# Key and value pieces of a dilated attention: two of eight multiplied on VectorE from PSUM instead of on GpSimd, and the second softmax's transposes placed two quarters later

## The chip, the core and the metric

The kernel runs on one core of a Trainium2 chip. The metric is device time in microseconds (us) of one execution.

## What is computed

One inference step of a two-layer decoder (one convolution layer, one attention layer, an MLP behind each) on 256 prompt tokens and 8 sequences of 8 sampled tokens, all in fp32. The attention layer has three head groups with (window, dilation) of (128, 1), (512, 4) and (2048, 16); the sampled tokens also read a key-value cache of 2048 past positions. Cut to the part that matters:

```
def dilated_group_sample(q, k_cat, v_cat, n_past, window, dilation):
    idx = n_past + jnp.arange(S)[:, None] - dilation * jnp.arange(n_keys)[None, :]
    kg = k_cat[:, idx_c]
    vg = v_cat[:, idx_c]
    s = jnp.einsum('bshe,bsnhe->bhsn', q, kg)
    ...
    p = jnp.exp(s - lse)
    o = jnp.einsum('bhsn,bsnhe->bshe', p.astype(vg.dtype), vg)

def merge_groups(outs, lses, dtype):
    w = jax.nn.softmax(jnp.stack(lses), axis=0)
    return jnp.sum(w[..., None] * jnp.stack(outs), axis=0).astype(dtype)
```

With dilation 16 each sampled query has 16 cached keys of its own that it shares with no other query of its sequence, so its scores and its weighted sum of values are not a matrix product with a shared operand: they are a product element by element and a sum.

## The kernel before

**Weights.** Every fp32 weight tile is loaded by SP into a ring `raw` and split into two fp32r halves: ScalarE copies the high part (`wh`, line 126), VectorE subtracts to get the low part (`wl`, line 127). `mm3` then issues three matmuls of 128x320 for each 128x128 weight block (lines 146 to 148). A split makes half of a raw tile, 128x1024; splits are emitted three halves ahead of the matmuls that use them, and the ring of halves has four places.

**The attention stage** is one list of steps that is sorted by a position. The unit is a quarter: twelve matmuls of 128x320. One head's query, key and value projections take 36 quarters, and this is called a frame; frame h holds `qkv_steps(h)` (the projections of head h), `scores2(h)` (its dilation-16 keys) and `side(h - 1)` (everything else of the attention of head h-1). After the eight heads comes one more frame, in which `side(7)` runs beside the first half of the output projection (`wo_steps`). The stage runs from about 1340 to 2200 us. The order of each engine's instructions is the order of that list: an instruction whose input is late holds all behind it on its engine. The second part of a step with a TensorE part (its `post`) is emitted after the next TensorE step.

**The dilation-16 pieces.** Keys and values of one head are each eight pieces of 128x1024 (one per sequence). `piece` places three things: the transfer into one of four buffers `al` at 2.9 quarters ahead, GpSimd's work at its position (a broadcast of one row `R` to all partitions, line 643, and a multiply, line 644) and VectorE's sum over it (line 649) 4.5 quarters later. The rows come from `row`, four small transfers (line 661). Key pieces stand 2.2 quarters apart from position 9 of their frame, value pieces from position 26.6, so the latter run over into the next frame.

**The two softmaxes.** `side` handles prompt rows in two halves: `p_s` makes scores, takes the maximum `mx` (line 753) and normalises (lines 618 to 620, the last two a reciprocal on VectorE and a scaling on ScalarE), `p_t` transposes the result on TensorE (line 761), `p_o` multiplies with the values. For sampled rows `s_soft` takes the maximum `mn` (line 821), and `s_t` and `n_t` transpose (lines 829 and 842). The transposes, the value transposes `v_t`, the scores `new_s` and some others each take one of three PSUM buffers named `s` for a moment; the sample's output product has the one buffer `o`.

## Time and profile before

| | |
|---|---|
| median of three executions | 3119.97 us (3115.67 to 3120.29) |
| the profiled execution | 3116.45 us, span 3114.7 us |
| TensorE, VectorE, ScalarE, GpSimd busy over the span | 95%, 63%, 43%, 27% |
| attention stage, one frame with side work | 97 to 98 us |
| in such a frame: TensorE, VectorE, GpSimd busy | 87, 88 and 74 us |

The shares over the whole span hide what the stages are like: GpSimd's pieces all lie in the attention stage, and VectorE, idle a third of the time elsewhere, is busy there for some nine tenths. Matmuls overlap, so that TensorE's busy time in a stretch is the time in which at least one is under way.

### The profile page before, as it was taken

How to read it: one execution, taken by the hardware profiler on the slowest of the kernel's cores; microseconds unless marked ns; L12 is line 12 of the kernel's file. 1: busy time of each engine (PE TensorE's matmuls, PEld its weight loads, DVE VectorE, ACT ScalarE, POOL GpSimd, SP SyncE). 2: the span in 40 equal slices, each digit the busy share in tenths (PEclk: the TensorE clock that was granted, in tenths of full speed). 3: DMA queues.
4: the chain of work that ended last, by engine and by line, in shares of the span. 5: the costliest groups of instructions: out<-in, count | busy, mean ns of one | idle time of the engine just before them, and what ended most of it. 6: DMA issues, size and time to landing. Idle time of an engine off the chain costs nothing.

```text
span 3114.7 us, 47460 instructions
## 1 busy us (share of the span) xinstructions
PE 2960.2 (95%) x19600; PEld 2897.2 (93%) x19608; DVE 1950.0 (63%) x2258; ACT 1341.0 (43%) x1889; POOL 828.7 (27%) x469
## 2 busy tenths in 40 slices
PE   6999799999999999999898898988999999999998
PEld 6998799999999999999888888877999999999998
DVE  7988854444444444567998888988644444444444
ACT  7877644334334334434334443334532333433442
POOL 2767200000000000034787777876100000000000
PEclk9999899999999999999999999999999999999999
DMA  5443244444444444466776667765444444444442
GB/s 189 146 139 122 96 149 150 150 151 152 152 151 151 149 149 149 149 211 213 260 260 240 253 234 259 257 235 207 146 151 150 149 149 149 149 149 149 149 149 88
DMA packets 96521, 533.62 MB, mean 171 GB/s; under 512 B 13809, under 2 KB 21233, under 8 KB 43825
## 3 DMA queue, kind: packets, MB, share of 16 engines
q1 hardware_dynamic: 92624, 526.54, 48.3%
q10 hardware_dynamic: 3600, 3.57, 0.3%
q8 instruction: 153, 2.51, 0.3%
q14 instruction: 64, 0.52, 0.0%
q0 software_dynamic: 80, 0.49, 0.0%
HBM read 517.33 MB, written 12.70 MB: 170 GB/s over the span
## 4 chain that ended last, share of the span: by engine, by line
PE 80%; DVE 10%; ACT 4%; issue 3%; POOL 2%; DMA 1%; SPq 0%; DVEq 0%; ACTq 0%; POOLq 0%
PE mm L148 25%; PE mm L146 25%; PE mm L147 25%; DVE wl L127 5%; ACT wh L126 1%; PE o L859 1%; POOL al L644 1%; DVE tv L649 1%; POOL pacc L378 1%; DMA al<-v 1%; DVE tk L649 0%; PE mm L368 0%; PE s L774 0%; POOL al L643 0%; ACT prod L377 0%
## 5 line engine op out<-in xcount | busy, mean ns | idle before, releaser
L127 DVE TENSOR_TENSOR wl<-raw,wh 128x1024 fp32r<-128x1024 f32 (+1 forms) x852 | 1213.8, 1431 | 727.2 <-ACT wh L126 727.1
L126 ACT ACTIVATE wh<-raw 128x1024 fp32r<-128x1024 f32 (+1 forms) x852 | 895.0, 1054 | 1478.2 <-PE mm L147 1298.5
L146 PE MATMUL mm<-bh,wh 128*128 128x320 f32 x3200 | 999.3, 312 | 11.9 <-ACT wh L126 11.9
L148 PE MATMUL mm<-bh,wl 128*128 128x320 f32 x3200 | 992.0, 310 | 13.6 <-DVE wl L127 13.5
L147 PE MATMUL mm<-bl,wh 128*128 128x320 f32 x3200 | 990.4, 310 | 0.0
L146 PE MATMUL mm<-ah,wh 128*128 128x320 f32 x2896 | 899.6, 311 | 32.7 <-ACT wh L126 12.6
L148 PE MATMUL mm<-ah,wl 128*128 128x320 f32 x2896 | 897.0, 310 | 3.8 <-DVE wl L127 3.7
L147 PE MATMUL mm<-al,wh 128*128 128x320 f32 x2768 | 855.2, 309 | 7.7 <-DVE al L154 4.0
L148 PEld LDWEIGHTS mm<-bh,wl 128*128 128x128 f32 x3200 | 605.1, 189 | 18.5 <-DVE wl L127 17.7
L146 PEld LDWEIGHTS mm<-bh,wh 128*128 128x128 f32 x3200 | 606.2, 189 | 16.3 <-ACT wh L126 12.2
L147 PEld LDWEIGHTS mm<-bl,wh 128*128 128x128 f32 x3200 | 605.9, 189 | 3.1
L146 PEld LDWEIGHTS mm<-ah,wh 128*128 128x128 f32 x2896 | 547.2, 189 | 39.1 <-ACT wh L126 14.4
L148 PEld LDWEIGHTS mm<-ah,wl 128*128 128x128 f32 x2896 | 547.1, 189 | 6.3 <-DVE wl L127 5.6
L147 PEld LDWEIGHTS mm<-al,wh 128*128 128x128 f32 x2768 | 521.1, 188 | 10.8 <-DVE al L157 5.4
L644 POOL TENSOR_TENSOR al<-al 128x1024 f32<-128x1024 f32 x128 | 360.7, 2818 | 96.2 <-DMA al<-k 50.4
L643 POOL PARTITION_BROADCAST al<-R x128 | 239.3, 1869 | 119.0 <-DMA R<-qT 89.8
L540 POOL DMA_DIRECT2D cb<-cb x1 | 0.7, 682 | 1011.7 <-PE mm L148 1011.7
L1016 POOL TENSOR_TENSOR bh<-bh,r 128x640 f32<-128x640 f32 x2 | 4.2, 2140 | 903.2 <-ACT r L1013 903.2
L378 POOL TENSOR_TENSOR pacc<-pacc,prod 128x320 f32<-128x320 f32 x168 | 181.0, 1113 | 76.0 <-ACT prod L377 75.1
L514 DVE TENSOR_TENSOR x<-x,mm 128x320 f32<-128x320 f32 x128 | 62.4, 487 | 178.8 <-PE mm L148 178.8
L509 DVE SCALAR_TENSOR_TENSOR sg<-mm,r 128x320 f32<-128x320 f32 x126 | 61.8, 492 | 162.4 <-PE mm L148 162.1
L388 DVE SCALAR_TENSOR_TENSOR s<-bl,wdw,s 128x320 f32<-128x320 f32 x272 | 130.0, 545 | 0.4 <-DMA out_cp<-gl 0.3
(205 smaller groups left out, 1715.0 us busy)
## 6 DMA issues: line engine op xcount, KB each, us to landing
raw<-w SPq DMA_DIRECT2D x252, 1024.0 KB
raw<-qkv SPq DMA_DIRECT2D x72, 1024.0 KB
raw<-pw SPq DMA_DIRECT2D x32, 1024.0 KB
al<-k SPq DMA_DIRECT2D x64, 512.0 KB
al<-v SPq DMA_DIRECT2D x64, 512.0 KB
raw<-k SPq DMA_DIRECT2D x16, 1024.0 KB
raw<-v SPq DMA_DIRECT2D x16, 1024.0 KB
raw<-pw2b SPq DMA_DIRECT2D x12, 1024.0 KB
```

The source lines that it names most:

```text
L126: act.activation(wh[:, :n], r, AF.Copy)
L127: dve.tensor_sub(wl[:, :n], r, wh[:, :n])
L146: pe.matmul(ps, wh, xh, start=start, stop=False)
L147: pe.matmul(ps, wh, xl, start=False, stop=False)
L148: pe.matmul(ps, wl, xh, start=False, stop=stop)
L378: pool.tensor_add(pa, pa, pr_)
L388: dve.scalar_tensor_tensor(a, win(f, k), dw(f, k), a, op0=OP.mult, op1=OP.add)
L509: dve.scalar_tensor_tensor(t, ps, 0.0, norm.r, op0=OP.max, op1=OP.mult)
L514: dve.tensor_add(x[:, ob], x[:, ob], ps)
L643: pool.partition_broadcast(wide, E2[kind, h, b // 4][32 * (b % 4):32 * (b % 4) + 1, :])
L644: pool.tensor_mul(t, t, wide)
L649: dve.tensor_reduce(E2["sum", kind, h][:, 8 * b:8 * b + 8], t.rearrange("p (a c) -> p a c", a=8), axis=AX.X, op=OP.add)
```

## The change

Pieces 2 and 5 of the eight (`BY_PE`) no longer go to GpSimd. Their row is sent as two rows, a high and a low part in fp32r; TensorE multiplies them with a 2x128 block of ones (two matmuls of 128x512, line 655 of the changed kernel), which spreads their sum to 128 partitions of two `s` buffers, and VectorE multiplies the piece by each (two 128x512 instructions, line 659). VectorE's total follows 1.5 quarters after the piece's position instead of 4.5. The other six pieces stand 2.9 quarters apart (2.6 in the last head) instead of 2.2 (2.1). A piece is fetched 3.6 quarters ahead, or right after the total that frees its buffer.

To have high and low parts, the query and the softmax weights get one ScalarE copy and one VectorE subtraction more per head. The mask of `new_s` is added by a matmul, and ScalarE copies the result, where VectorE added the mask. Positions in `side` move: `p_t` of the second half from 13.6 and 13.9 to 15.6 and 15.9, behind `s_t` and `n_t`; both `p_o`, `pv`, `s_red` and `s_out` 0.4 to 1.5 later; the `v_t` one quarter apart instead of 0.3.

```diff
+        BY_PE = (2, 5)
...
+            ends.append(at + (1.5 if b in BY_PE else 4.5))
+            j = 32 * (b % 4)
...
+            def on_pe(c):
+                box = {}
+
+                def go():
+                    box["ps"] = ps = s_tile()
+                    pe.matmul(ps, onesr[j:j + 2], E2[kind, h, b // 4].bitcast(F32R)[j:j + 2, 512 * c:512 * c + 512],
+                              start=True, stop=True)
+
+                def post():
+                    dve.tensor_mul(t[:, 512 * c:512 * c + 512], t[:, 512 * c:512 * c + 512], box["ps"])
+                add(at + .3 * c, go, post)
...
-            add(at - 2.9, None, fetch)
-            add(at, None, mult)
-            add(at + 4.5, None, total)
+            add(max(at - 3.6, ends[n - 4] + .01 if n > 3 else 0), None, fetch)
+            if b in BY_PE:
+                on_pe(0)
+                on_pe(1)
+            else:
+                add(at, None, mult)
+            add(ends[n], None, total)
+
+        def pieces(kind, h, t0, dt):
+            i = 0
+            for b in range(NB):
+                piece(kind, h, b, t0 + dt * (i - .5 if b in BY_PE else i))
+                i += b not in BY_PE
...
+                if b in BY_PE:
+                    sp.dma_start(r[32 * j:32 * j + 1, :], hi[8 * b:8 * b + 8, :].bitcast(F32))
+                    sp.dma_start(r[32 * j + 1:32 * j + 2, :], lo[8 * b:8 * b + 8, :].bitcast(F32))
+                else:
+                    sp.dma_start(r[32 * j:32 * j + 1, :], src[8 * b:8 * b + 8, :])
...
-            for b in range(NB):
-                piece("k", h, b, t0 + 9 + 2.2 * b)
+            pieces("k", h, t0 + 9, 2.9)
...
+                    pe.matmul(ps[:64, :NNEW], idb[:, :64], cb[:, B_MN:B_MN + NNEW], start=True, stop=False)
...
-                    dve.tensor_add(S[:, NKEY:], E["new"][:64, :NNEW], cst[:64, C_MN:C_MN + NNEW])
-                    dve.tensor_reduce(E["m"][:, 0:1], S[:, NKEY:], axis=AX.X, op=OP.max)
+                    act.activation(S[:, NKEY:], E["new"][:64, :NNEW], AF.Copy)
+                    dve.tensor_reduce(E["m"][:, 0:1], E["new"][:64, :NNEW], axis=AX.X, op=OP.max)
...
+            def weights():
+                p = E["S"][:, NPE:NKEY]
+                ph = ap.tile([64, 128], F32R, name="qT")
+                pl = ap.tile([64, 128], F32R, name="ql")
+                split_in(ph, pl, p)
...
-                v_t(.3 * g, g)
+                v_t(g, g)
...
-            p_t(6.4, 0, 0)
+            p_t(6.8, 0, 0)
...
-            p_t(13.6, 1, 0)
-            p_t(13.9, 1, 3)
             s_t(14.6, 0, 5)
             n_t(14.9)
-            p_o(17, 1)
-            t2, dt = (13.5, 2.1) if last else (26.6, 2.2)
...
+            p_t(15.6, 1, 0)
+            p_t(15.9, 1, 3)
+            p_o(18.5, 1)
+            step(12.5 if last else 22, None, weights)
+            step(13 if last else 30, None, lambda: row("v", h, 1, *E2["p", h]))
+            pieces("v", h, t0 + (14.5 if last else 26.4), 2.6 if last else 2.9)
```

Two places of the order show what this does around the second softmax of a full frame. First TensorE, before the change: the second `p_t` (line 761, six transposes of `Sp` in two PSUM buffers), one quarter, then `s_t` (line 829) and `n_t` (line 842). `mm` rows are the projections; the bracket names the engine whose work the instruction waits for.

```order
L761 MATMUL s<-cst,Sp 128x128 [waits Activation_49]
L761 MATMUL s<-cst,Sp 128x128 x2
L761 MATMUL s<-cst,Sp 128x128 [waits DVE_49,PE_49]
L761 MATMUL s<-cst,Sp 128x128 x2
...
L829 MATMUL s<-cst,S 128x64 [waits DVE_49]
L829 MATMUL s<-cst,S 128x64 x4
L842 MATMUL s<-cst,S 64x64 [waits Activation_49]
L842 MATMUL s<-cst,S 64x64 x2
```

The same place on TensorE in the changed kernel: first the two spreading matmuls of key piece 2 (line 655), a quarter, `s_t` (line 864) and `n_t` (line 877), a quarter, and then the second `p_t` (line 796).

```order
L655 MATMUL s<-R,ones 128x512 [waits DMAHW6_49,DMAHW5_49]
L655 MATMUL s<-R,ones 128x512 [waits DVE_49]
...
L864 MATMUL s<-cst,S 128x64 [waits Activation_49]
L864 MATMUL s<-cst,S 128x64 x4
L877 MATMUL s<-cst,S 64x64 [waits DVE_49]
L877 MATMUL s<-cst,S 64x64 x2
...
L796 MATMUL s<-cst,Sp 128x128 [waits Activation_49]
L796 MATMUL s<-cst,Sp 128x128 x2
L796 MATMUL s<-cst,Sp 128x128 [waits DVE_49]
L796 MATMUL s<-cst,Sp 128x128 x2
```

`p_t` has moved behind `n_t`, and `n_t`, which waited for ScalarE, now waits for VectorE: of the three `s` buffers it gets the one that the first spreading matmul of line 655 filled, which VectorE's multiply of line 659 empties.

Next VectorE before the change, from the sample's maximum `mn` on: two splits (`wl`), the second softmax's `mx` and reciprocal, the total of a value piece (`tv`), a finished projection (`v`), the head before's output (`os`, `ah`), and the total of a key piece (`tk`).

```order
L821 TENSOR_REDUCE mn<-m 64x1 [waits DVE_49]
L619 RECIPROCAL l<-l 64x1 [waits Activation_49]
L127 TENSOR_TENSOR wl<-raw,wh 128x1024 [waits DMAHW1_49,PE_49,Activation_49]
L753 TENSOR_REDUCE mx<-o 128x1 [waits PE_49]
L619 RECIPROCAL l<-l 128x1 [waits Activation_49]
L649 TENSOR_REDUCE tv<-al 128x8 [waits Pool_49]
L127 TENSOR_TENSOR wl<-raw,wh 128x1024 [waits PE_49,Activation_49]
...
L886 TENSOR_TENSOR os<-os,tv 128x64 [waits DVE_49]
L154 TENSOR_TENSOR ah<-os,ah 128x64 [waits Activation_49]
L649 TENSOR_REDUCE tk<-al 128x8 [waits Pool_49]
L127 TENSOR_TENSOR wl<-raw,wh 128x1024 [waits DMAHW2_49,PE_49,Activation_49]
```

And the same stretch of VectorE in the changed kernel.

```order
L665 TENSOR_REDUCE tv<-al 128x8 [waits Pool_49]
L856 TENSOR_REDUCE mn<-m 64x1 [waits DVE_49]
L620 RECIPROCAL l<-l 64x1 [waits Activation_49]
L127 TENSOR_TENSOR wl<-raw,wh 128x1024 [waits DMAHW7_49,PE_49,Activation_49]
L788 TENSOR_REDUCE mx<-o 128x1 [waits PE_49]
L620 RECIPROCAL l<-l 128x1 [waits Activation_49]
L127 TENSOR_TENSOR wl<-raw,wh 128x1024 [waits PE_49,Activation_49]
...
L154 TENSOR_TENSOR ah<-os,ah 128x64 [waits Activation_49]
L665 TENSOR_REDUCE tk<-al 128x8 [waits Pool_49]
L659 TENSOR_TENSOR al<-al,s 128x512 [waits DMAHW3_49,PE_49]
L127 TENSOR_TENSOR wl<-raw,wh 128x1024 [waits DMAHW0_49,Activation_49]
L659 TENSOR_TENSOR al<-al,s 128x512 [waits PE_49]
```

The total `tv` has moved from behind the second reciprocal to ahead of `mn`, and the two multiplies of key piece 2 stand behind `tk` and around the next split; the first of them also waits for the transfer of its piece.

## Rows read from the trace of the kernel before

**Rows 1.** The page: busy time of each engine over the span, and GpSimd's line of the 40 slices of the span (a slice is 77.9 us, a digit its busy share in tenths).

```profile
PE 2960.2 (95%) x19600; PEld 2897.2 (93%) x19608; DVE 1950.0 (63%) x2258; ACT 1341.0 (43%) x1889; POOL 828.7 (27%) x469
...
POOL 2767200000000000034787777876100000000000
```

**Rows 2.** Busy time by stretch: the frame of the first side work, the next frame, and a stretch of the last head. Columns: the stretch, its length, busy us and instructions of each engine, granted clock, DMA share, GB/s.

```profile
1423.00:1509.00 86.00, 83.75 (x563) 80.15 (x562) 73.25 (x68) 41.13 (x57) 57.59 (x24) 1.00 0.75 269
1515.00:1612.00 97.00, 86.94 (x555) 81.29 (x555) 87.68 (x77) 39.76 (x57) 73.80 (x32) 0.96 0.68 245
...
2122.00:2172.00 50.00, 39.46 (x242) 35.95 (x240) 41.26 (x44) 22.14 (x30) 37.03 (x16) 0.91 0.61 232
```

**Rows 3.** TensorE's timeline, the scores of the new keys (line 713), which stand at position 2.4 of each frame with side work. Columns here and in every timeline: start, duration, engine, line, operation, out<-in, shape, count, and in brackets the idle time before and what ended it.

```profile
1423.25 0.56 PE L713 MATMUL s<-k,q 128*64 128x64 f32 x6
1509.07 0.56 PE L713 MATMUL s<-k,q 128*64 128x64 f32 x6
...
2093.35 0.45 PE L713 MATMUL s<-k,q 128*64 128x64 f32 x4 [4.14 <-DVE q L941]
```

**Rows 4.** The waits of all engines from 1515 to 2121 us (six frames): total, times, longest.

```profile
POOL al L644 <- DMA al<-k: 47.2, 15, 7.4
...
DVE wl L127 <- ACT wh L126: 37.0, 34, 2.5
...
PE s L761 <- ACT Sp L620: 30.1, 6, 5.4
...
POOL al L644 <- DMA al<-v: 23.7, 8, 4.1
...
PE mm L148 <- DVE wl L127: 13.9, 12, 1.7
```

**Rows 5.** VectorE's timeline through the sample softmax and the second prompt softmax of one frame.

```profile
1635.18 0.14 DVE L821 TENSOR_REDUCE mn<-m 64x1 f32<-64x4 f32 x1
1636.58 0.15 DVE L619 RECIPROCAL l<-l 64x1 f32<-64x1 f32 x1 [1.26 <-ACT S L618]
1638.85 1.39 DVE L127 TENSOR_TENSOR wl<-raw,wh 128x1024 fp32r<-128x1024 f32 x1 [2.12 <-ACT wh L126]
...
1642.17 0.16 DVE L619 RECIPROCAL l<-l 128x1 f32<-128x1 f32 x1 [1.06 <-ACT Sp L618]
1642.25 1.20 DVE L649 TENSOR_REDUCE tv<-al 128x8 f32<-128x1024 f32 x1
1644.28 3.08 DVE L127 TENSOR_TENSOR wl<-raw,wh 128x1024 fp32r<-128x1024 f32 x1 [0.83 <-ACT wh L126]
...
1648.93 1.21 DVE L649 TENSOR_REDUCE tk<-al 128x8 f32<-128x1024 f32 x1
```

**Rows 6.** TensorE's timeline over the same stretch.

```profile
1638.05 0.31 PE L147 MATMUL mm<-bl,wh 128*128 128x320 f32 x1
1638.20 0.31 PE L148 MATMUL mm<-bh,wl 128*128 128x320 f32 x1
1643.36 1.22 PE L761 MATMUL s<-cst,Sp 128*128 128x128 f32 x6 [4.85 <-ACT Sp L620]
...
1645.17 0.47 PE L146 MATMUL mm<-bh,wh 128*128 128x320 f32 x1
1645.43 0.47 PE L147 MATMUL mm<-bl,wh 128*128 128x320 f32 x1
...
1649.18 0.35 PE L842 MATMUL s<-cst,S 64*64 64x64 f32 x3 [1.18 <-ACT Sp L764]
```

**Rows 7.** Groups of instructions by line and shape, 1440 to 2121 us (seven frames). Columns: line, engine, operation, out<-in, shapes, count | busy us, mean ns of one | idle before, and what ended it.

```profile
L127 DVE TENSOR_TENSOR wl<-raw,wh 128x1024 fp32r<-128x1024 f32 x194 | 384.5, 2003 | 42.0 <-ACT wh L126 42.0
L644 POOL TENSOR_TENSOR al<-al 128x1024 f32<-128x1024 f32 x112 | 314.7, 2810 | 92.3 <-DMA al<-k 47.8 <-DMA al<-v 24.5 <-DVE wl L127 6.0
...
L859 PE MATMUL o<-wl,zz 128*128 128x512 f32 x70 | 22.2, 398 | 0.0
...
L866 DVE TENSOR_TENSOR Sp<-o,cst 128x1024 f32<-128x1024 f32 x7 | 8.4, 1207 | 0.0
...
L811 DVE TENSOR_TENSOR S<-s,S 64x512 f32<-64x512 f32 x7 | 4.9, 694 | 0.2
...
L811 DVE TENSOR_TENSOR S<-s,S 64x128 f32<-64x128 f32 x8 | 2.3, 293 | 0.2
```

**Rows 8.** The same view for 2230 to 2400 us, where GpSimd does nothing (its slices in the page): the same split.

```profile
L127 DVE TENSOR_TENSOR wl<-raw,wh 128x1024 fp32r<-128x1024 f32 x49 | 60.0, 1225 | 60.8 <-ACT wh L126 60.8
```

**Rows 9.** VectorE's and GpSimd's timelines over one stretch: four splits in a row, and the pieces that GpSimd worked on meanwhile.

```profile
1713.74 9.27 DVE L127 TENSOR_TENSOR wl<-raw,wh 128x1024 fp32r<-128x1024 f32 x4 [0.51 <-ACT wh L126]
...
1711.99 2.41 POOL L644 TENSOR_TENSOR al<-al 128x1024 f32<-128x1024 f32 x1
...
1716.73 3.10 POOL L644 TENSOR_TENSOR al<-al 128x1024 f32<-128x1024 f32 x1
...
1722.16 3.11 POOL L644 TENSOR_TENSOR al<-al 128x1024 f32<-128x1024 f32 x1
```

**Rows 10.** The last head: first and last of GpSimd's sixteen instructions on its value pieces, and TensorE's longest wait from 2121 to 2205 us (total, times, longest).

```profile
2132.17 1.29 POOL L643 PARTITION_BROADCAST al<-R  x1 [17.91 <-DVE x L967]
...
2168.19 2.35 POOL L644 TENSOR_TENSOR al<-al 128x1024 f32<-128x1024 f32 x1
...
PE s L761 <- ACT Sp L620: 6.0, 1, 6.0
```

More of the change, by code (lines that the diff above doesn't have):

```diff
@@ L69 @@
 C_SEL = 192
-C_MN = 200
-C_N = C_MN + NNEW
+C_N = 200
 B_ID = 0
@@ L74 @@
 B_MP = B_MS + NPE
-B_N = B_MP + 1152
+B_MN = B_MP + 1152
+B_N = B_MN + NNEW
 CV_TAPS = {14: (11, 12), 15: (11, 12)}
@@ L541, in decoder_step @@
         idb = cb[:, B_ID:B_ID + 128]
+        onesr = ones.bitcast(F32R)
         B = {}
@@ L628, in decoder_step @@
         E2 = {}
-        slots = [0]
+        ends = []
+        BY_PE = (2, 5)
         def piece(kind, h, b, at):
-            n = slots[0]
-            slots[0] += 1
+            n = len(ends)
             t = spread[:, n % 4]
+            ends.append(at + (1.5 if b in BY_PE else 4.5))
+            j = 32 * (b % 4)
             def fetch():
@@ L650, in total, with row @@
                                   axis=AX.X, op=OP.add)
-            add(at - 2.9, None, fetch)
-            add(at, None, mult)
-            add(at + 4.5, None, total)
-        def row(kind, h, half, src):
+            add(max(at - 3.6, ends[n - 4] + .01 if n > 3 else 0), None, fetch)
[10 more added lines that the diff above has]
+                i += b not in BY_PE
+        def row(kind, h, half, src, hi, lo):
             r = E2[kind, h, half] = ap.tile([128, 1024], F32, name="R", bufs=2)
@@ L670, in post @@
                 q = ap.tile([64, 128], F32, name="qT")
-                act.activation(q, E2["qT", h][:64, :128], AF.Copy)
-                E2["q", h] = q
-                row("k", h, 0, q)
+                qh = ap.tile([128, 128], F32R, name="orr")
+                ql = ap.tile([64, 128], F32R, name="ql")
+                ps = E2["qT", h][:64, :128]
+                act.activation(q, ps, AF.Copy)
+                split_in(qh[:64], ql, ps)
+                E2["q", h] = q, qh[:64], ql
+                row("k", h, 0, *E2["q", h])
             add(t0 + 6, go, post)
-            add(t0 + 12, None, lambda: row("k", h, 1, E2["q", h]))
-            for b in range(NB):
-                piece("k", h, b, t0 + 9 + 2.2 * b)
+            add(t0 + 12, None, lambda: row("k", h, 1, *E2["q", h]))
+            pieces("k", h, t0 + 9, 2.9)
         def side(h, t0):
@@ L711, in go @@
                     E["new"] = ps = s_tile()
+                    pe.matmul(ps[:64, :NNEW], idb[:, :64], cb[:, B_MN:B_MN + NNEW], start=True, stop=False)
                     for g in range(G):
-                        pe.matmul(ps[:64, g * 64:g * 64 + 64], B[h, 0, g][:, SEQ:], B[h, 1, g][:, SEQ:], start=True,
-                                  stop=True)
+                        pe.matmul(ps[:64, g * 64:g * 64 + 64], B[h, 0, g][:, SEQ:], B[h, 1, g][:, SEQ:], start=False,
+                                  stop=(g == G - 1))
                 def post():
@@ L889, in side @@
             last = h == H - 1
+            def weights():
[3 more added lines that the diff above has]
+                split_in(ph, pl, p)
+                E2["p", h] = p, ph, pl
+                row("v", h, 0, *E2["p", h])
             for g in range(G):
-                v_t(.3 * g, g)
+                v_t(g, g)
             step(1.2, None, q_fill)
@@ L897, in side @@
             qk(1, 5.2, 6.2)
-            p_t(6.4, 0, 0)
+            p_t(6.8, 0, 0)
             qk(2, 7.2)
-            p_o(8.6, 0)
+            p_o(9, 0)
             p_s(9.2, 1)
             step(9.8, None, s_soft)
-            p_t(13.6, 1, 0)
-            p_t(13.9, 1, 3)
             s_t(14.6, 0, 5)
             n_t(14.9)
-            p_o(17, 1)
-            t2, dt = (13.5, 2.1) if last else (26.6, 2.2)
-            step(11.5 if last else 22, None, lambda: row("v", h, 0, E["S"][:, NPE:NKEY]))
-            step(11.5 if last else 30, None, lambda: row("v", h, 1, E["S"][:, NPE:NKEY]))
-            for b in range(NB):
-                piece("v", h, b, t0 + t2 + dt * b)
+            p_t(15.6, 1, 0)
[4 more added lines that the diff above has]
+            pieces("v", h, t0 + (14.5 if last else 26.4), 2.6 if last else 2.9)
             for t in range(5):
-                pv(18 + 2.2 * t, t)
-            step(28.3, None, s_red)
-            s_out(33.2)
+                pv(19 + 2.2 * t, t)
+            step(29.3, None, s_red)
+            s_out(34.2)
             if not last:
```

9 lines of the change are left out of this document (4 added, 5 removed).

## Prediction, made before the changed kernel was run

> **What bounds the kernel now.** I began with the page: TensorE is busy 95% of the span, VectorE 63%, GpSimd 27% [rows 1]. That would say TensorE, but GpSimd's line shows that all its pieces lie in slices 18 to 28, the attention stage, so the change acts there alone, and the question is what bounds that stage. The busy times by stretch answer it: in the first frame with side work TensorE is busy 83.75 of 86 us and VectorE 73.25; in the next TensorE 86.94 of 97 and VectorE 87.68 [rows 2]. The same mark, the scores of the new keys, stands 1509.07 − 1423.25 = 85.8 us apart at first, and then (2093.35 − 1509.07) / 6 = 97.4 us [rows 3]. So 85.8 us is what TensorE needs for a frame, and six frames take 11.6 us longer.
>
> Two readings are open: TensorE's waits add the 11.6 us, or VectorE sets the pace. Of TensorE's waits from 1515 to 2121 us the largest is the second `p_t` (line 761) for ScalarE's scaled softmax: 30.1 us in six times, 5 us a frame; waits for splits are 13.9 us, 2.3 a frame [rows 4]. The timelines show the place. VectorE takes `mn`, which the list puts at position 9.8, at 1635.18. TensorE's matmuls start 0.147 us apart until 1638.5, where it stops at position 13.6 [rows 6]; a quarter of twelve being 1.76 us, it was then near 11.7. The chain behind it (reciprocal, split, `mx`, reciprocal) has its last reciprocal at 1642.2 [rows 5], and TensorE goes on at 1643.36 after 4.85 us. Then its matmuls start 0.27 us apart (1645.17, 1645.43), for about a quarter: 12 x 0.12 or some 1.3 us more. VectorE reached `mn` late because its queue was behind, and its waits are small: 9.3 us a frame (97 − 87.68), of which 1.26 + 2.12 + 1.06 + 0.83 = 5.3 in this chain [rows 5]. I choose the second reading: VectorE with some 88 us of work and 9 of waits makes the 97, and TensorE's stop at `p_t` is where it is shown to be early. A shorter wait there gives nothing back unless VectorE has less to do.
>
> **The change, part by part, for one full frame.** All prices are from the grouped rows unless another group is named.
>
> *Multiplies on VectorE.* Four pieces of a head, two halves each: eight instructions of 128x512 with one operand in PSUM. The trace has no such instruction; nearest is line 866, 128x1024 with one operand in PSUM, 1207 ns, half of it 0.60 [rows 7]; upper bound line 811, 64x512 with PSUM and SBUF, 0.69. I take 0.62: +5.0 (4.8 to 5.5).
>
> *Splits of the row, the mask.* Two more subtractions of 64 rows and 128 columns at 0.29 (line 811, the 64x128 form), less one mask addition of about the same size or a little more: +0.3. ScalarE's copies lie beside it (it is busy 40 of 97 us).
>
> *What GpSimd takes from VectorE.* The split `wl` takes 2003 ns on average in the stage [rows 7] and 1225 where GpSimd does nothing [rows 8]. The excess, 194 x 0.778 = 151 us over 112 pieces, is 1.35 us of VectorE time a piece. In one stretch four splits take 9.27 us, 4.4 more than 4 x 1.225; three multiplies of GpSimd overlap that stretch by 0.7, 3.1 and 0.9 us, 4.6 in all [rows 9]. So a split seems to stand while GpSimd multiplies. Line 866, with one operand in PSUM, shows no stretch, though it too ran among the pieces. Other instructions with both operands in SBUF pay as well, so I take 1.45 a piece. Four pieces fewer: −5.8. Bounds: GpSimd's multiply is 2.81 us; at least half the average gain might be lost if the remaining pieces, no longer back to back, meet as many splits (−2.7); at most a split always stands the whole 2.81 (−11.2).
>
> By the Trainium skill ("SBUF — State Buffer", section "Who interferes with whom") a VectorE instruction with two SBUF inputs shares a read port with GpSimd and one waits for the other to finish, while one with at most one SBUF input never does. The stretch of four splits and line 866 agree with that; the rule would make each of the new multiplies free of this tax, as I priced them.
>
> *The order around `mn`.* Before, the total `tv` (1.20 us) filled a time in which VectorE had to wait for ScalarE anyway [rows 5]; behind the change it stands ahead of `mn`, and the time is empty: +1.2 (0 to 1.2).
>
> *`p_t` behind `n_t`.* `p_t` will hardly wait. But `n_t` needs the buffer that the first multiply of key piece 2 empties, and this multiply stands behind `mn`, reciprocal, split, `mx`, reciprocal, split, `os` and `tk`. In the rows of before `tk` begins at 1648.93 and takes 1.21, so the multiply ends about 15.5 us after `mn` (1635.18 + 15.6 = 1650.8), while TensorE gets to `n_t` one quarter and the small matmuls after its old stop, some 2 us later. So a wait of 5 becomes one of 6 to 9 us. Behind `n_t` are the projections, and so the emptied `wh` and `wl` halves that further splits need; with three halves of lead VectorE is not starved by 9 us of stop. A check that TensorE doesn't become the bound: from its scores' last part (position 8.2), which `mn` needs, to `n_t` it has 15 us of work and the chain takes 17, so its own loop is 85.8 + 2.0 for spreading (eight matmuls at about a quarter of a microsecond: two of line 859 in a row take 0.47) + some 2 to 4 = 90 to 92, below 97. I cost it at nothing; if that cover is gone, it is at most 9 − 5 = 4 us a frame.
>
> *The queue of SP.* Four more row transfers a head, in a queue with room; fetches lie as far ahead as before or a little less. Nothing, but see the third rival.
>
> Sum for a full frame: 5.0 + 0.3 − 5.8 + 1.2 = +0.7, and six of them: +4.2.
>
> *The first two frames* are TensorE's, with GpSimd in the way of nobody: twelve spreading matmuls at 0.25: +3 (0 to +5).
>
> *The last head.* There `p_t` waits 6.0 us and GpSimd's chain of eight value pieces runs from 2132.17 to 2170.5, 4.8 us a piece, without a pause [rows 10]. No key pieces come in that frame, so `n_t` has no such neighbour. Six pieces instead of eight end 9.6 us earlier, less 2 for a start one position later and behind more row transfers; VectorE gets 4 x 0.62 more and two pieces less of tax (−2.9). VectorE is busy 41.26 of 50 us there [rows 2], so some 7 to 8 us can be gained before it is full: −6.5 (0 to −9.6).
>
> All: 4.2 + 3 − 6.5 = **+0.7 us**. Against the profiled execution (3116.45) that is 3117; the profiled one lies 3.5 under the median (3119.97) and near the lowest. I predict 3117 us: a change that can't be told from none. A measurement of this kernel tells about 0.2%, 6 us, from no change.
>
> **Rivals.** *One: a spared piece is worth the whole multiply.* If a split stands at the head of VectorE's queue nearly whenever GpSimd multiplies, four pieces give 11.2 instead of 5.8: 0.7 − 5.4 = −4.7 a frame, −28, with +3 and −6.5 as above 3085. For it: the stretch of four splits. Against it: the mean of 1.35, about half of 2.81. Partial gains give what lies between.
>
> *Two: TensorE's stop at `p_t` was the loss.* Then 6 x 5.0 and 6 x 1.3 for the slow matmuls behind go, 38 us, with the last head's 6.5 less the 3 of the first frames: 3075. For it: this is TensorE's largest wait, and a frame without it takes 85.8. Against it: VectorE's 88 of 97, and the wait of `n_t`, which takes its place.
>
> *Three, slower: VectorE's multiplies meet late transfers.* GpSimd waited for key pieces 15 times (47.2 us, 3.1 each) and value pieces 8 times (23.7 us, 3.0 each) in six frames of 96 pieces [rows 4]. On GpSimd that cost nothing. Now the first multiply of a piece waits for its transfer on VectorE, with splits and both softmaxes behind. If all four are late as GpSimd's were, 12 us a frame; if one or two in four, 3 to 6, so +18 to +37: 3135 to 3154, around 3142. It decides once the fetch lands after VectorE has come to the multiply; piece 5, fetched only when the total of piece 1 has freed its buffer, is the likeliest. Against it: VectorE runs behind its positions, which gives a transfer time.
>
> *Four: it does nothing.* That is my forecast itself, by balance; that the multiplies stay hidden I hold for excluded, since VectorE has no free time of that size.
>
> **Chances and range.** Forecast 0.37 (3111 to 3124); rival one or a part of it 0.22 (3082 to 3111); rival two 0.13; rival three 0.28. Faster by over 0.2%: 0.22 + 0.13 = 0.35; within: 0.37; slower: 0.28. The range 3078 to 3148 leaves out most of rival two (0.10) and the far end of three (0.08).
>
> **What would show it.** Right: the wait at line 796 nearly gone, one at line 877 for line 659 of 6 to 9 us a frame; splits at about 1.85 us on average; line 659 at 0.6; frames 97 to 98.5 us apart; GpSimd done with the last head 6 to 8 us earlier. Rival one: frames of 92 and splits below 1.7. Rival two: frames of 91 to 92 with VectorE at 86 or less. Rival three: VectorE's line 659 waiting for `al` transfers, 3 us a time, and frames over 100. Most likely to be wrong is the 1.45, because it is an average over who happens to meet whom, and the claim that a longer stop of TensorE costs nothing.

## The result, and the profile after

The changed kernel takes 3159.3 us (3156.07 to 3160.23); the kernel before took 3117.82 us in the runs beside it. The ratio is 1.0134, with a 95% interval of 1.0116 to 1.0152: some 41 us slower, above the predicted range, which ended at 3148. The profiled execution has a span of 3157.2 us, 42.5 more than before. Its page, the busy time of each engine, to be read against [rows 1]:

```profile
PE 2995.8 (95%) x19672; PEld 2918.0 (92%) x19680; DVE 1930.6 (61%) x2330; ACT 1343.3 (43%) x1913; POOL 662.5 (21%) x405
```

VectorE has 19 us less to do than before, GpSimd 166 less, TensorE 36 more. So the relief came, and the kernel is slower all the same. The marks show where. In TensorE's timeline the scores of the new keys (line 713 before, 748 after) start at, in the changed kernel:

```profile
1425.99 0.51 PE L748 MATMUL s<-k,q 128*64 128x64 f32 x6
1520.36 0.51 PE L748 MATMUL s<-k,q 128*64 128x64 f32 x6
...
2130.24 0.51 PE L748 MATMUL s<-k,q 128*64 128x64 f32 x6
```

and the last of them in the kernel before (the row at 2093.35 in [rows 3] is the remainder of this one, behind a wait; its start should have been used there, and gives 96.6 us a frame instead of 97.4):

```profile
2088.88 0.33 PE L713 MATMUL s<-k,q 128*64 128x64 f32 x2
```

Up to the first mark the changed kernel is 2.7 us later, the first frame with side work takes 94.4 instead of 85.8 us (+8.6), the next six 101.6 instead of 96.6 (+30.1 together), and what follows the last mark 1.1 more. That is all of the 42.5.

Busy time by stretch, five full frames each (the windows run from mark to mark; columns as in [rows 2]), the kernel before:

```profile
1509.07:1996.26 487.19, 438.29 (x2801) 412.42 (x2805) 440.11 (x381) 198.76 (x285) 374.29 (x161) 0.97 0.69 248
```

and the changed kernel:

```profile
1520.36:2031.43 511.07, 454.76 (x2846) 420.91 (x2851) 430.44 (x424) 199.81 (x300) 274.48 (x121) 0.95 0.65 237
```

Per frame VectorE went from 440.11 / 5 = 88.0 us of work and 9.4 of idle time to 86.1 of work and 16.1 idle. The forecast let both together grow by 0.7 us. What VectorE waits for, and the largest wait of TensorE, over the same five frames (total, times, longest):

```profile
DVE wl L127 <- ACT wh L126: 48.5, 36, 2.2
...
PE s L877 <- DVE al L659: 37.1, 5, 8.2
...
DVE al L659 <- DMA al<-v: 1.4, 1, 1.4
```

`p_t` (line 761 before) has vanished from the list, and `n_t` (line 877) waits 7.4 us a frame for VectorE's multiply. VectorE in turn waits 9.7 us a frame for ScalarE's half of the splits, where it was 28.9 / 5 = 5.8. The timelines of one frame show the stop. VectorE from `mn` to the multiply, as [rows 5]:

```profile
1647.69 0.14 DVE L856 TENSOR_REDUCE mn<-m 64x1 f32<-64x4 f32 x1
...
1654.57 0.95 DVE L788 TENSOR_REDUCE mx<-o 128x1 f32<-128x768 f32 x1
1656.58 0.16 DVE L620 RECIPROCAL l<-l 128x1 f32<-128x1 f32 x1 [1.06 <-ACT Sp L619]
1658.69 1.91 DVE L127 TENSOR_TENSOR wl<-raw,wh 128x1024 fp32r<-128x1024 f32 x1 [1.95 <-ACT wh L126]
...
1660.92 1.96 DVE L921 TENSOR_TENSOR os<-os,tv 128x64 f32<-128x64 f32 x1
1663.20 0.23 DVE L154 TENSOR_TENSOR ah<-os,ah 128x64 fp32r<-128x64 f32 x1 [0.32 <-ACT ah L153]
1663.35 1.21 DVE L665 TENSOR_REDUCE tk<-al 128x8 f32<-128x1024 f32 x1
1664.47 0.68 DVE L659 TENSOR_TENSOR al<-al,s 128x512 f32<-128x512 f32 x1
```

and TensorE, as [rows 6]:

```profile
1657.22 0.52 PE L864 MATMUL s<-cst,S 64*128 64x64 f32 x5
1665.21 0.53 PE L877 MATMUL s<-cst,S 64*64 64x64 f32 x3 [7.47 <-DVE al L659]
```

From `mn` to the end of the multiply VectorE needs 17.5 us, and TensorE stands at `n_t` for 7.47 of them with its transposes of line 796 still behind it, whose input follows the reciprocal at 1656.58 by one scaling on ScalarE.

Where in the frame the time goes is seen when it is cut at two marks: `n_t` on TensorE, and the last finished projection `q` of the next head on VectorE, about position 4. One stretch from `n_t` to `q` and the one from there to the next `n_t` (columns as in [rows 2]), the kernel before:

```profile
1746.93:1805.79 58.86, 55.73 (x368) 52.86 (x369) 56.46 (x46) 23.23 (x32) 44.63 (x19) 1.00 0.69 254
1805.79:1843.62 37.83, 31.33 (x194) 28.75 (x193) 30.80 (x31) 16.52 (x26) 29.34 (x14) 0.95 0.73 254
```

and the changed kernel:

```profile
1766.14:1831.10 64.96, 61.05 (x381) 56.50 (x381) 58.18 (x54) 22.38 (x33) 38.31 (x17) 0.96 0.61 215
1831.10:1869.59 38.49, 29.71 (x191) 27.31 (x191) 30.25 (x34) 17.57 (x27) 16.03 (x7) 0.92 0.73 266
```

On average over five of each, the stretch from `q` to `n_t`, which holds the stop, takes 38.5 us before and 38.2 after. The stretch behind the stop, from `n_t` to `q`, takes 58.9 and 64.3, with TensorE busy 55.9 and 61.2 us of it: the loss lies there.

### The profile page after: what moved, and what is told of

Same layout as the page of the kernel before. It is cut to its first block, busy times and chain, and to the rows that moved or that the text cites. A ratio compares the mean times of both kernels' runs of the same rounds, so it can differ in the third digit from the quotient of the medians.

```text
span 3157.2 us, 47707 instructions
## 1 busy us (share of the span) xinstructions
PE 2995.8 (95%) x19672; PEld 2918.0 (92%) x19680; DVE 1930.6 (61%) x2330; ACT 1343.3 (43%) x1913; POOL 662.5 (21%) x405
## 4 chain that ended last, share of the span: by engine, by line
PE 81%; DVE 8%; ACT 3%; DMA 3%; issue 2%; POOL 2%; SPq 0%; DVEq 0%; ACTq 0%; POOLq 0%
PE mm L146 25%; PE mm L148 25%; PE mm L147 25%; DVE wl L127 3%; ACT wh L126 1%; PE o L894 1%; POOL al L648 1%; DMA raw<-qkv 1%; DMA al<-k 1%; DMA R<-qT 1%; POOL pacc L378 1%; DVE tv L665 1%; POOL al L647 1%; PE mm L368 0%; DVE tk L665 0%
## 5 line engine op out<-in xcount | busy, mean ns | idle before, releaser
L127 DVE TENSOR_TENSOR wl<-raw,wh 128x1024 fp32r<-128x1024 f32 (+1 forms) x852 | 1144.9, 1349 | 768.5 <-ACT wh L126 768.2
L146 PE MATMUL mm<-bh,wh 128*128 128x320 f32 x3200 | 1006.2, 314 | 12.5 <-ACT wh L126 11.5
L146 PE MATMUL mm<-ah,wh 128*128 128x320 f32 x2896 | 899.8, 311 | 30.8 <-ACT wh L126 12.9
L146 PEld LDWEIGHTS mm<-bh,wh 128*128 128x128 f32 x3200 | 608.1, 190 | 28.9 <-issue 12.6
L148 PEld LDWEIGHTS mm<-bh,wl 128*128 128x128 f32 x3200 | 607.5, 190 | 13.2 <-DVE wl L127 12.9
L147 PEld LDWEIGHTS mm<-al,wh 128*128 128x128 f32 x2768 | 521.7, 189 | 10.5 <-DVE al L157 5.3
L648 POOL TENSOR_TENSOR al<-al 128x1024 f32<-128x1024 f32 x96 | 258.8, 2696 | 186.5 <-DMA al<-k 81.3
L647 POOL PARTITION_BROADCAST al<-R x96 | 176.2, 1835 | 233.8 <-DMA R<-qT 142.1
```

Of the source, the lines that this page charges most:

```text
L127: dve.tensor_sub(wl[:, :n], r, wh[:, :n])
L146: pe.matmul(ps, wh, xh, start=start, stop=False)
L147: pe.matmul(ps, wh, xl, start=False, stop=False)
L148: pe.matmul(ps, wl, xh, start=False, stop=stop)
L647: pool.partition_broadcast(wide, E2[kind, h, b // 4][j:j + 1, :])
L648: pool.tensor_mul(t, t, wide)
```

## The experiments

Each kernel is given with its median and the ratio to the kernel before, measured beside it (3117.6 to 3120.0 us, so rows measured at different times compare to some 2 us); "frame" is the mean of five full frames of its profile, "work" and "idle" are VectorE's in such a frame.

| kernel | us | ratio (95%) | frame | work | idle |
|---|---|---|---|---|---|
| before | 3117.8 | 1 | 97.4 | 88.0 | 9.4 |
| changed | 3159.3 | 1.0134 (1.0116 to 1.0152) | 102.2 | 86.1 | 16.1 |
| x1_by35: pieces 3 and 5 | 3145.7 | 1.0095 (1.0069 to 1.0122) | 99.0 | 86.1 | 12.9 |
| x2_sched: positions only | 3139.8 | 1.0070 (1.0055 to 1.0085) | 100.8 | 89.8 | 11.0 |
| x3_oldpt: pieces, `p_t` in front | 3172.2 | 1.0167 (1.0152 to 1.0182) | 104.0 | 88.2 | 15.8 |
| x4_drop: two pieces left out | 3092.2 | 0.9913 (0.9898 to 0.9928) | 94.7 | 84.4 | 10.3 |
| x5_by35_oldpt | 3156.9 | 1.0124 (1.0107 to 1.0140) | 101.8 | 88.2 | 13.6 |
| z1_share: `n_t` without a buffer | 3150.9 | 1.0099 (1.0080 to 1.0118) | 100.5 | 86.1 | 14.4 |
| z6_end: changed, `os` later | 3152.9 | 1.0107 (1.0086 to 1.0129) | 101.0 | 87.8 | 13.3 |
| z5_sched_end: x2 and `os` later | 3127.2 | 1.0025 (1.0016 to 1.0035) | 97.6 | 89.9 | 7.7 |
| y1_soft: before, `mn` behind `mx` | 3113.1 | 0.9984 (0.9975 to 0.9994) | 95.7 | 87.3 | 8.4 |
| y1b_soft_end: and `os` later | 3098.2 | 0.9944 (0.9927 to 0.9961) | 93.5 | 87.4 | 6.1 |
| w3_sched_both: y1b with the positions | 3118.7 | 1.0002 (0.9991 to 1.0013) | 96.7 | 90.4 | 6.2 |
| w6_pieces_both: y1b with the pieces | 3125.3 | 1.0019 (1.0009 to 1.0030) | 97.1 | 86.6 | 10.5 |
| z2_soft_end: changed with both moves | 3132.0 | 1.0046 (1.0030 to 1.0062) | 98.0 | 86.7 | 11.3 |
| y2_all: z2, pieces 3 and 5, old `p_t` | 3138.6 | 1.0062 (1.0043 to 1.0081) | 99.1 | 87.9 | 11.2 |
| w5_drop_both: y1b, two pieces left out | 3068.8 | 0.9843 (0.9822 to 0.9864) | 89.6 | 83.5 | 6.1 |

VectorE's work lies between 83.5 and 90.4 us in all of them; what parts most of them is its idle time, 6 to 16 us.

### Is it the stop at `n_t`, and whose is it?

x1_by35 takes the multiply away from `n_t`'s buffer:

```diff
-        BY_PE = (2, 5)
+        BY_PE = (3, 5)
```

> The changed kernel with pieces 3 and 5 instead of 2 and 5 on TensorE and VectorE, so that key piece 2's spreading (position 13.35) becomes key piece 3's at 16.25, behind the second transposes; n_t then takes no buffer that VectorE's multiply must empty. Theory A (the shared PSUM buffer makes TensorE stop 7.4 us at n_t, and TensorE sets the pace of the frame): that wait is under 1 us, frames 95 to 97 instead of 102, total 3110 to 3130. Theory B (TensorE's stop is only where VectorE's lag shows, and the added work makes the frame longer): another wait of 5 us or more takes its place, frames 100 or more, total 3145 to 3160.

It is 14 us faster than the changed kernel, and nearer to theory B: the total lies at the lower edge of its range, the frame a little below. The wait at `n_t` is gone, as theory A had it, and another takes its place: the second transposes wait 5.3 us a frame for ScalarE's copy of `n_t` (line 881):

```profile
PE s L796 <- ACT pn L881: 26.6, 5, 6.3
```

x2_sched has no pieces on TensorE at all, only the moved positions, the mask and the parts of the row:

```diff
-        BY_PE = (2, 5)
+        BY_PE = ()
...
-            pieces("k", h, t0 + 9, 2.9)
+            pieces("k", h, t0 + 9, 2.2)
...
-            pieces("v", h, t0 + (14.5 if last else 26.4), 2.6 if last else 2.9)
+            pieces("v", h, t0 + (14.5 if last else 26.6), 2.1 if last else 2.2)
```

> The changed kernel with all pieces on GpSimd again at 2.2 quarters: of the change only the moved positions (second transposes behind s_t and n_t), the mask on TensorE and the row parts remain. Theory A: TensorE's stop for the second softmax nearly goes with nothing in its place, frames 92 to 94, total 3080 to 3100. VectorE as the bound of the whole frame (the reading in the prediction): frames stay at 97, total 3112 to 3124.

Both theories were wrong: it is 21 us slower than before. With `p_t` behind `n_t` and no multiply in the way, a stop of 5 us became one of 6.1, and ScalarE's timeline says why:

```profile
1655.71 1.04 ACT L126 ACTIVATE wh<-raw 128x1024 fp32r<-128x1024 f32 x1
1660.99 0.26 ACT L153 ACTIVATE ah<-os 128x64 fp32r<-128x64 f32 x1 [4.24 <-DVE os L921]
...
1662.42 0.31 ACT L881 ACTIVATE pn<-s 64x192 f32<-64x192 f32 x1
1662.63 0.47 ACT L799 ACTIVATE Sp<-s 128x384 f32<-128x384 f32 x1
```

The copy `pn` that empties `n_t`'s buffer stands behind the copy `ah` of the head before, which waits 4.24 us for VectorE's `os`, a step at position 48.5 of its own head, which is 12.5 of this frame. So TensorE's transposes, ready long before, wait for an instruction of another head through two queues. That this stop is what costs the 21 us is not shown: VectorE's work is also 1.8 us a frame more, no run moves `p_t` alone, and w3 below loses as much with the stop gone.

x3_oldpt leaves the pieces as in the change and puts `p_t` back in front:

```diff
-            s_t(14.6, 0, 5)
-            n_t(14.9)
-            p_t(15.6, 1, 0)
-            p_t(15.9, 1, 3)
-            p_o(18.5, 1)
+            p_t(13.6, 1, 0)
+            p_t(13.9, 1, 3)
+            s_t(14.6, 0, 5)
+            n_t(14.9)
+            p_o(17, 1)
```

> The changed kernel with the second transposes back at 13.6 and 13.9, ahead of s_t and n_t, and p_o at 17. Theory A: the second half of these transposes needs a buffer that the multiply of key piece 2 must empty, so the stop moves there and keeps 7 to 10 us; frames 102 to 105, total 3155 to 3180. If the new place of the transposes itself were the loss: frames 97 to 99, total 3118 to 3140.

Time and frame lie in theory A's ranges, but the trace doesn't bear out its reason. TensorE's waits at the second transposes, five frames:

```profile
PE s L796 <- ACT Sp L799: 20.3, 5, 5.1
...
PE s L796 <- ACT Sp L621: 10.6, 5, 2.4
```

They wait 2.1 us a frame for the softmax and 4.1 for ScalarE's copy of their own first half, 6.2 together, less than the 7 to 10 expected. That copy stands behind `ah`, which waits for `os`, as in x2; in the frame looked at TensorE goes on at 1665.88, and the multiply of key piece 2 only begins at 1666.75. So the stop moved to the next instruction that needs a buffer, but not for the multiply's sake; why this kernel is 13 us slower than the changed one stays open. z1_share asks the same from the other side, with `n_t` in the columns that `s_t` leaves free:

```diff
-                    E["nt"] = ps = s_tile()
+                    E["nt"] = ps = E["st", 0][:, 320:]
```

> The changed kernel, n_t written to the unused columns of s_t's PSUM buffer, so that it needs none of its own. Theory C (TensorE is held by the buffer that the multiply of key piece 2 empties): n_t no longer waits, and the second transposes, next in the list, wait for the same multiply instead, 4 to 6 us; frames 99 to 101 instead of 102, total 3135 to 3153. If the wait at n_t were a loss by itself that goes with it: frames 95, total 3105 to 3120.

```profile
PE s L796 <- DVE al L659: 29.3, 10, 5.7
```

The wait, now 5.9 us a frame, moved to line 796 as foretold, here for VectorE's multiply, and 8 us were won. x5_by35_oldpt takes x1's edit and x3's together:

> The changed kernel with pieces 3 and 5 on TensorE (no multiply between n_t and its buffer) and the second transposes back at 13.6 and 13.9, p_o at 17. Theory C (a frame is two phases in series: TensorE's from n_t to position 4 of the next frame, and VectorE's queue from there until the buffers and the second softmax are released): the second softmax and n_t are done some 14 us behind mn as in the kernel before, frames 97 to 98.5, total 3125 to 3140. Theory D (the place of the transposes makes no difference once the buffer is free): as with pieces 3 and 5 and the new places, frames 99.4, total 3140 to 3150.

Neither, and worse than either: the chain behind `mn` took its 14 us as foretold, yet frames are 101.8. VectorE there waits for transfers of key pieces (9.4 us in five frames, 0 in the changed kernel), which accounts for 2 of the 3 to 5 us; the rest is not explained.

### What clears the stop

Two edits, here in the kernel before, go to the cause of the stop, VectorE's and ScalarE's queues:

```diff
-            step(9.8, None, s_soft)
+            step(10.1, None, s_soft)
...
-                step(48.5, None, s_end)
+                step(53, None, s_end)
```

y1_soft has the first alone, which puts `mx` and the second softmax ahead of `mn`; y1b_soft_end (y1b for short) has both.

> The kernel before with the sample softmax at 10.1 instead of 9.8, which puts mn behind mx and the second softmax in VectorE's and ScalarE's queues. Theory C: TensorE's stop at the second transposes falls from 5 us to under 1, the chain from mn (or mx) to n_t from 14 to 9 or 10 us, frames 93 to 95, total 3090 to 3107. If VectorE's sum of work alone sets the frame (the reading of the prediction): the stop shrinks, but frames stay at 96 to 97.5, total 3110 to 3122.

> As the one before, and the step that ends the head before (os, then ScalarE's copy that waits for it) moved from position 48.5 to 53, behind n_t. Theory C: ScalarE's 4 us wait for os no longer stands ahead of the copy of the transposes, n_t comes 2 to 4 us earlier, frames 91 to 93.5, total 3075 to 3097. VectorE's sum alone: no change against the run before it.

TensorE's waits in y1_soft, five frames:

```profile
PE s L842 <- ACT Sp L764: 20.9, 5, 5.2
...
PE s L761 <- ACT Sp L620: 6.0, 5, 1.6
```

and in y1b_soft_end:

```profile
PE s L761 <- ACT Sp L620: 6.1, 5, 1.7
PE s L842 <- ACT Sp L764: 3.2, 5, 0.6
```

with, by stretch:

```profile
1511.83:1979.42 467.59, 433.76 (x2806) 408.25 (x2805) 437.06 (x379) 196.76 (x285) 378.17 (x160) 0.98 0.72 259
```

With the first edit alone the total fell into the range of the reading it was to refute: the wait at `p_t` falls from 5 to 1.2 us a frame, but `n_t` then waits 4.2 for ScalarE's copy of the transposes (before: 0.9); the total is only just faster. With the second that falls to 0.6, and the kernel is 19.4 us faster than before, 1 us above the range: the best of those that compute everything. So a stop of TensorE in this place costs time, and VectorE's sum of work alone doesn't set the frame: it is 87.4 us, hardly less than before, and the frame is 3.9 us shorter, 3.3 of it idle time of VectorE.

The second edit alone, on the changed kernel and on x2:

> The changed kernel with os of the head before (and ScalarE's copy that waits for it) moved from 48.5 to 53, out of the queue ahead of the multiply of key piece 2. Theory C: the multiply comes 2.5 to 3.5 us earlier, the wait at n_t falls from 7.4 to 4 or 5, frames 99 to 100, total 3135 to 3147. If TensorE's added work alone makes the frame: same as the changed kernel, 3155 to 3161.

> All pieces on GpSimd, moved positions (the run that was 21 us over the kernel before), and os at 53. In that run the second transposes waited 6.3 us a frame for ScalarE's copy of n_t, which stood behind the copy that waits for os. Theory C: that wait falls to 1 or 2 us, frames 96 to 97, total 3105 to 3120. If the moved transposes cost in another way: 3130 to 3145.

In z5 the wait for `pn` fell from 6.1 to 1.6 us as expected and 12.6 us came back, 7 us short of the range. In z6 the wait at `n_t` fell from 7.4 to 4.6 as expected, but the frame lost 1.2 instead of 2 to 3, and the total is 6 us above its range. From `q` to `n_t` the frame is 3.3 us shorter there, but behind `n_t`, where `os` now stands, 1.9 us longer.

### What the pieces cost where the stop is gone

z2 is the changed kernel with both edits.

> The changed kernel with mn behind mx (10.1) and os at 53, the two moves that made the kernel before 19 us faster. Theory C: n_t waits for the multiply still, but less (4 to 5 us), frames 97 to 99, total 3115 to 3140, above the kernel before with the same moves (3098). If the spared GpSimd work pays once the queue is clear: total 3085 to 3100.

With both edits the wait at `n_t` is 1.9 us a frame, and the changed kernel is still 34 us above y1b. Three more kernels divide that. w3 is x2 with both edits. w6 is the changed kernel with both edits, x3's edit and the other positions as before:

```diff
-                v_t(g, g)
+                v_t(.3 * g, g)
...
-            p_t(6.8, 0, 0)
+            p_t(6.4, 0, 0)
...
-            p_o(9, 0)
+            p_o(8.6, 0)
...
-                pv(19 + 2.2 * t, t)
-            step(29.3, None, s_red)
-            s_out(34.2)
+                pv(18 + 2.2 * t, t)
+            step(28.3, None, s_red)
+            s_out(33.2)
```

and w5 is y1b with this (x4 is the kernel before with it):

```diff
-            add(at, None, mult)
+            if b not in (2, 5):
+                add(at, None, mult)
```

> All pieces on GpSimd, moved positions, and both moves that clear the queue (mn behind mx, os at 53): it differs from the changed kernel with both moves (3132) by the pieces alone and from the kernel before with both moves (3098) by the moved positions alone. If the pieces on TensorE and VectorE cost by themselves, through TensorE's 2.8 us of spreading a frame and VectorE's idle time behind it: 3105 to 3118. If the moved positions (value transposes one quarter apart among them) are what is left: 3125 to 3135.

> The changed kernel with both moves, and all other positions (v_t 0.3 apart, the second transposes at 13.6 and 13.9, p_o, pv, s_red, s_out) as before the change: the pieces alone. If the pieces cost by themselves: 3122 to 3138, no better than with the moved positions. If the moved positions cost: 3098 to 3112.

> The kernel before with both moves, and without the broadcast and multiply of pieces 2 and 5 (left out, as in the run at 3092): what the relief of GpSimd is worth at most where the queue is clear. VectorE's work falls by 3.5 us a frame as there; if its idle time stays at 6 us a frame: 3068 to 3082. If TensorE's own 86 us and its waits for splits then hold: 3085 to 3098.

Against y1b the moved positions cost 20.5 us (w3; a hair above the first range), the pieces 27.1 (w6, in its first range), both together 33.8 (z2). Both w3 and w6 also have the mask on TensorE and the row's two parts, so their sum counts these twice; no run has them alone. To do nothing for pieces 2 and 5 gains 29.4 (w5, in its first range). So doing them on TensorE and VectorE, with the mask, the row's parts and the wider spacing that come with it, costs 3125.3 − 3068.8 = 56.5 us, 7 us a head, and GpSimd's share that it spares is worth 29. In x4_drop, the same test in the kernel before, the relief is 26 us:

> The kernel before without the broadcast and multiply of pieces 2 and 5 (their product is left out, the total sums the raw piece). It prices what GpSimd's quarter takes from the others. Theory A: only what falls between position 4 and the softmax counts, TensorE's stop at the second transposes shrinks from 5 to 2 or 3 us, frames 94 to 95, total 3095 to 3105. VectorE as the bound of the whole frame: four pieces at 1.45 to 2.3 us less, frames 88 to 92, total 3065 to 3085.

It came out between the two ranges, just below the first; the stop at the second transposes only shrank from 5.0 to 4.4 us. VectorE's work fell there by 88.0 − 84.4 = 3.6 us a frame, 0.9 a piece. Busy time by stretch of w6, five frames:

```profile
1518.23:2003.55 485.32, 458.11 (x2851) 417.38 (x2851) 432.83 (x423) 202.81 (x300) 257.47 (x121) 0.98 0.69 250
```

and w5:

```profile
1509.18:1957.19 448.01, 428.40 (x2806) 406.81 (x2805) 417.51 (x381) 198.34 (x286) 286.08 (x122) 0.98 0.76 270
```

TensorE's busy time is 91.6 us a frame in w6 and 85.7 in w5, VectorE's 86.6 and 83.5: TensorE, with 91.6 of 97.1, has become the fuller of the two, and VectorE's work went up by only 3.1 though the multiplies are 5.4. The three kernels without pieces on TensorE in which the stop is gone, y1b, w3 and w5, have the same idle time of VectorE, 6.1 to 6.2 us, and their frames follow its work: 87.4, 90.4 and 83.5 us of work, 93.5, 96.7 and 89.6 us of frame. Between `n_t` and `q` VectorE is busy 60.8 of 61.2, 63.6 of 64.5 and 58.4 of 58.9 us in them. So VectorE does set the pace there once no stop is in the way, and w3's loss goes with its 3 us more of work: 2.8 for splits that take longer (2061 ns instead of 1969), 1.4 for the row's subtractions less the mask, and 1.1 less for `os` and `ah`. With the pieces on TensorE the idle time is 10.5 to 11.3 again. And in w6 VectorE's multiplies wait for key pieces, 2.8 us a frame:

```profile
DVE al L659 <- DMA al<-k: 13.8, 5, 2.8
```

The last kernel, y2, is the changed one with both edits, x1's and x3's:

> The changed kernel with pieces 3 and 5, the transposes at their old places, and both moves of the two runs before. Theory C: VectorE's phase shrinks as in those, TensorE's phase keeps its extra 2.8 us of spreading and the waits for v_t's copies, frames 94 to 96, total 3095 to 3115, no better than the kernel before with the two moves. VectorE's sum alone: its 2.5 us a frame less show, and it ends 10 to 20 us under the kernel before with the two moves.

It is at least 23 us above both theories' ranges: these multiplies wait 15.5 us in five frames for transfers, and TensorE 23.8 us for splits (7.5 in z2). Which of the two leads to the other I did not separate.

## Why the prediction failed, step by step

**Which engine sets the pace.** The step that failed is "a shorter wait there gives nothing back unless VectorE has less to do", and with it "I cost it at nothing" for the longer stop at `n_t`. y1b has VectorE's work within 0.6 us and gains 19.4 us; the changed kernel has less of it and loses 41. The terms for VectorE's work were not the trouble: 5.0 + 0.3 − 5.8 = −0.5 us a frame forecast, −1.9 measured. VectorE's work sets the frame only on top of an idle time that the stops make, and that I had taken as fixed. The chain of work in the rest of a frame, kernel before (start, duration, engine and line):

```profile
1675.94 0.37 PE o L859 x2
1676.32 1.12 DVE tk L649
1677.44 1.27 DVE wl L127
...
1683.51 5.39 DVE wl L127 x2
```

and at the same place behind the stop of the changed kernel:

```profile
1678.16 0.94 PE o L894 x4
1679.10 0.66 PE s L655 x2
...
1697.63 0.93 PE o L894 x4
...
1712.29 0.81 PE s L910 x6
```

Before, the path leaves TensorE some 27 us behind `n_t` and goes along VectorE's totals and splits; after, it stays with TensorE, but for one total and one split at 1691.82, to 1715, that is 50 us behind `n_t`. TensorE, which reaches `n_t` as long after `q` as before (38.2 us) and then has 5.2 us more to do, is the late one there, and VectorE, which can be only three halves ahead, waits for the halves to come free: 7.1 us of idle time between `n_t` and `q`, 2.4 before. It isn't returned: from `q` to the multiply VectorE's queue is the late one again.

An estimate of TensorE's 5.2 us, from rows: three spreading pairs at 0.66 us are 2.0; the second `p_t`, now behind `n_t`, is some 0.7; and sixteen more matmuls a frame (24 instead of 8) run slowly, 0.27 us apart instead of 0.147, which is 1.9. The slow ones follow TensorE's stops, at `n_t` and at ScalarE's copies `vn` (2.7 us of waits a frame, none before); the granted clock of the stretch is 0.96 instead of 1.00 in the rows of the section on the result. Before, the stop lay at `p_t`, and most of the slow matmuls behind it fell ahead of `n_t`.

My check of TensorE's loop (90 to 92 us) let VectorE's part begin at position 8.2 with 17 us; but its queue is behind from position 4, where in the changed kernel it last waits for TensorE (`q` at 1627.02) and needs 38 us to the multiply at 1665.1, in which TensorE has 30 us of work. So the two stretches add up, 38 us of VectorE's queue and 64 that TensorE's work fills, and a frame is 102 us where the check had TensorE at 92 at most.

**The wait at `n_t`.** Forecast 6 to 9 us, measured 7.4; the place and the reason were right, the price wrong. The stretch that holds the wait is no longer than before; what it costs comes behind it, by the estimate above in TensorE's work left over and its slow matmuls.

**Multiplies.** Grouped rows of the changed kernel, 1440 to 2150 us (columns as in [rows 7]):

```profile
L127 DVE TENSOR_TENSOR wl<-raw,wh 128x1024 fp32r<-128x1024 f32 x194 | 321.6, 1674 | 71.0 <-ACT wh L126 70.9
...
L659 DVE TENSOR_TENSOR al<-al,s 128x512 f32<-128x512 f32 x56 | 37.5, 677 | 4.6 <-DMA al<-v 4.6
...
L154 DVE TENSOR_TENSOR ql<-S,qT 64x128 fp32r<-64x128 f32 x7 | 8.6, 1222 | 0.0
```

677 ns instead of 0.62: +5.4 a head, within the bounds. By the Trainium skill ("SBUF — State Buffer", section "Who interferes with whom") such an instruction, with one input in PSUM, is not held by GpSimd, and the row agrees: all 56 took 669 to 696 ns, nearly the 694 of line 811 in [rows 7], while the split still takes 1674.

**Splits of the row.** Forecast 0.29 us each, from a row of line 811, which has one operand in PSUM. The query's subtraction has that too and took 0.27; the one of the softmax weights has both operands in SBUF and took 1.22, so with the mask addition of 0.34 gone this term is +1.2 instead of +0.3. It is stretched as the splits are, which I had read from them and not applied here.

**What GpSimd takes from VectorE.** Forecast 1.45 us a piece, of which 1.35 for the splits; over the 28 splits of a head that would have brought their mean to 1.81 us (the 1.85 written down does not follow from it). It fell to 1674 ns, 9.1 us a head or 2.3 a piece. But that is not the price of a piece: leaving the pieces out took the mean only to 1904 and VectorE's work down by 0.9 a piece. The longer frame is not the reason for the rest either: w6, whose frame of 97.1 us is as long as the 97.4 before, has nearly the same mean.

```profile
L127 DVE TENSOR_TENSOR wl<-raw,wh 128x1024 fp32r<-128x1024 f32 x140 | 234.8, 1693 | 16.3 <-ACT wh L126 16.2
```

GpSimd has six pieces in x4 as in w6. What differs is that they stand 2.9 quarters apart in w6 and 2.2, with gaps, in x4, and that VectorE spends 5.3 us a frame on multiplies that GpSimd doesn't stretch; which of the two does it no run here shows.

**TensorE's spreading.** Forecast 0.25 us a matmul from rows of line 859. A pair holds TensorE for 0.66 us in the chain above (1679.10 to 1679.76), so 2.6 us a head instead of 2.0; and it is on the path now.

**The first frame.** It is TensorE's, as forecast, but its 8.6 us were put at some 2: beside the spreading stand a wait of 3.1 us at `n_t`, also here, and slow matmuls behind it (granted clock 0.96 over that frame, 1.00 in [rows 2]).

**The last head.** Forecast −6.5, measured +1.1. `p_t` no longer waits there, but the six pieces are not back to back any more: GpSimd waits for their transfers, and so does VectorE's multiply.

```profile
2178.36 2.39 POOL L648 TENSOR_TENSOR al<-al 128x1024 f32<-128x1024 f32 x1 [2.91 <-DMA al<-v]
...
2191.34 2.50 POOL L648 TENSOR_TENSOR al<-al 128x1024 f32<-128x1024 f32 x1 [3.94 <-DMA al<-v]
...
2206.60 3.39 POOL L648 TENSOR_TENSOR al<-al 128x1024 f32<-128x1024 f32 x1 [5.47 <-DMA al<-v]
```

and VectorE:

```profile
2181.49 0.69 DVE L659 TENSOR_TENSOR al<-al,s 128x512 f32<-128x512 f32 x1 [4.31 <-DMA al<-v]
```

GpSimd's second, fourth and sixth piece wait 2.9, 3.9 and 5.5 us, VectorE 4.3: a piece is fetched only when an earlier total has freed its buffer, and stands in SP's queue behind ten row transfers instead of eight.

**The rivals.** One and two, both faster, were wrong as forecasts of this change, though one's sign, splits below 1.7 us, came; but rival two's reading, that TensorE's stop is a loss, is the one that y1b bears out, with a gain of 19.4 us where I had 38. Rival three had the right sign for a wrong reason: VectorE's multiplies waited for transfers only 1.4 us in the five frames. It was true in w6, y2 and the last head.

## What to carry to other kernels

Before a long instruction is put on an in-order engine, look who needs the buffer that it empties: with three buffers in turn the waiting just goes to the next user, and four kernels here (x1, x2, x3, z1) moved the stop and kept 5 to 6 us of it. A stop is cleared at the queue that it waits for: two positions, a row maximum taken first and an unrelated step moved away, were worth 19.4 us. A frame here is two stretches in series, in which different engines are late: work spared in the one does not pay for work added in the other. The chain of work tells which engine is late at which place.
